# A convolution summed in PSUM, and comparison tables in PSUM

## The chip, the cores and the metric

The kernel runs on one core of a Trainium2 chip. The number is the device time of one execution in microseconds. Five engines work side by side, each through its own queue in order: PE (matrix multiply; its weight loads are listed as PEld), DVE (vector), ACT (activations), POOL (GpSimd), and SP, which here only issues DMAs. SBUF is the working memory. [...]

## The reference, cut to what matters

The input is one sequence of 512 tokens of width 1024. Block one has a mixer and an FFN, block two has attention branches, a cross attention and a product-key expert layer. The change touches the mixer and the expert layer's routing:

```python
# mixer: stick-breaking attention over 8 heads of 64, and beside it
c = glu_a * jax.nn.sigmoid(glu_b)
c = causal_depthwise_conv(c, conv_dw_w[layer], conv_dw_b[layer])   # 31 taps, 512 channels
c = jax.nn.silu(layer_norm(c, conv_ln_g[layer], conv_ln_b[layer]))
mixed = jnp.concatenate([attn, c], axis=-1) @ w_out[layer]
```

In the expert layer each token takes, for each of 8 heads, the 16 best of 128 x 128 expert pairs (i, j) from two lists of 128 keys. With a softmax over the 16 scores as weights w, the output is the weighted sum over the chosen experts of gelu(x . u) v.

## The kernel before, in words

Activations lie transposed, features on partitions and 512 tokens along the free dimension. Weights stream from HBM in chunks of 128 x 1024 (class `Stream`, L47): SP loads one, ACT rounds it to `whi` (L70), POOL subtracts to get `wlo` (L74), and `mm3` (L134) multiplies three times, hi x hi, hi x lo and lo x hi. This POOL subtraction runs through the whole kernel.

**Mixer (L300).** PE's order is written by hand (L498 to L514); a planner places the instructions of the other engines. In iteration j PE does a GEMM of `fills` (24 matmuls), then the `rest` of the fill before it (L430: column sums `misc`, of which DVE's L162 and others make the norm; L415: a transpose of V). From j = 7 it adds the scores `z` of one unit (L449, then a mask, L450, for each of two heads) and the `tail` of the unit before (L479), which needs `sbe` and `splo` from DVE (L459, L466). `weigh` (L485) follows each fourth unit. The depthwise convolution is done by DVE tap by tap (`conv_steps`, L375) in the background: 27 taps for each of four channel blocks, three further taps go to ACT and POOL. `self.bg(TAPS)` places five of them per iteration, `self.bg(TAPS0)` four in the first ones. Then come the layer norm and silu of the convolution (L533 to L558), beside the first half of the output projection. The PSUM banks are: 2 for `mm`, 4 for `z`, 1 `misc`, 1 `av`.

**Routing (L1273).** For 16 key blocks PE makes queries and scores `psc`, from which DVE takes the best 16 (L1285 to L1289). Then, for each 128 tokens, `choose` (L1338) picks the 16 best pairs and looks their keys up (`pick`, L1328). For three of the four token blocks `gates` (L1422) turns that into a 128 x 128 table of weights per token: `onehots` (L1406) compares the column numbers `iota` with i and j for four tokens, J on DVE (L1411), two columns of I on DVE and scaled by ACT (L1416), two compared and scaled in one DVE instruction each (L1418). PE multiplies J and I to `pg` (L1439), and ACT copies that out. Three calls are made ahead (AHEAD). Between such steps PE works on expert blocks (`stored_block`, L1481, 24 matmuls of 384 columns), in an order set by the costs that the generators yield; POOL also gathers rows for the first 128 tokens (L1234), of which DVE takes products (L1248). The PSUM banks are: 2 `mm`, 1 `tr`, 5 `psc`/`pg`. The last stage, `combine` (L1486), sums the experts.

Of the kernel before, what the change touches and what calls it, by code (L numbers as in the profile page):

```python
# [30 lines left out]
TAPS = 5  # L31
# [64 lines left out]
class Kernel:  # L96
# [58 lines left out]
    def rsq(self, out, ss, scale, eps, work, const=1.0, n=512, parts=P, tags=("rsq_y", "rsq_t"), bufs=1):  # L155

        nc = self.nc
        y = work.tile([P, 512], F32, name="rsq_y", tag=tags[0], bufs=bufs)[:parts, :n]
        t = work.tile([P, 512], F32, name="rsq_t", tag=tags[1], bufs=bufs)[:parts, :n]
# [140 lines left out]
    def mixer(self):  # L300
        tc, nc, a = self.tc, self.nc, self.a
        g1 = self.g["norm1_g"]
        with tc.tile_pool(name="mx", bufs=1) as mp, tc.tile_pool(name="mxp", bufs=1, space=PSUM) as pp:
# [8 lines left out]
            nlnb = mp.tile([P, 4], F32, name="nlnb")  # L312
            nc.vector.tensor_scalar(nlnb, lnb, -1.0, None, op0=ALU.mult)
# [46 lines left out]
            def conv_steps(cb):  # L360

                c = conv[:, cb, :]
# [14 lines left out]
                if OFF:  # L377
                    nc.vector.tensor_tensor(c, c, acc, op=ALU.add)
# [63 lines left out]
            def score(b, sb):  # L442
# [42 lines left out]
            def weigh(b):  # L485
                av = pp.tile([P, S], F32, name="av", tag="av", bufs=1)
# [11 lines left out]
            with tc.manual_schedule(engines={mybir.EngineType.PE}):  # L498
                for j in range(FIRST + len(units)):
                    after = fills[j][0](*fills[j][1:]) if j < len(fills) else None  # L500
                    if rest:
                        rest()
                    rest, i = after, j - FIRST
                    if i < -1:
                        self.bg(TAPS0)
                        continue
# [26 lines left out]
            pm = pp.tile([P, S], F32, name="misc", tag="misc", bufs=1)  # L533
# [4 lines left out]
            for cb in range(4):  # L538
# [3 lines left out]
                if cb == 0:  # L542
                    pv = pp.tile([P, S], F32, name="misc", tag="misc", bufs=1)
# [729 lines left out]
    def route(self, ep, rp, pp):  # L1273
# [3 lines left out]
        iota = rp.tile([P, P], F32, name="iota")  # L1277
        nc.gpsimd.iota(iota, pattern=[[1, P]], base=0, channel_multiplier=0, allow_small_or_imprecise_dtypes=True)
# [13 lines left out]
        for b in range(16):  # L1292
            ps = self.gemm("pq", self.xg)
            if b == 0:
                pr = pp.tile([P, S], F32, name="tr", tag="tr", bufs=1)
                self.sums(pr, [self.ssq], self.ones)
                self.rsq(self.rstd, pr, 1.0 / D, EPS, rp, tags=("ut", "ut"), bufs=AHEAD + 1)
            q = rp.tile([P, S], F32, name="pq", tag="pq", bufs=AHEAD + 1)
            nc.vector.tensor_tensor(q, ps, self.rstd, op=ALU.mult)
            pc = pp.tile([P, 4, P], F32, name="psc", tag="psc", bufs=5)  # L1300
# [4 lines left out]
            if b < 8:  # L1305
                t = rp.tile([P, S], F32, name="ut", tag="ut", bufs=AHEAD + 1)
# [31 lines left out]
        def choose(tb):  # L1338
# [59 lines left out]
            pt = pp.tile([P, 3, P], F32, name="tr", tag="tr", bufs=1)  # L1398
# [3 lines left out]
            nc.vector.tensor_copy(t, pt)  # L1402
            T[tb] = t
# [297 lines left out]
```

## Time and profile before

| | us |
|---|---|
| median of 3 runs (lowest, highest) | 2563.18 (2561.69, 2563.8) |
| the profiled execution, its span | 2565.2, 2563.4 |
| PE busy | 2429.5 (95%) |
| DVE busy | 2003.0 (78%) |
| POOL busy, of that the subtraction L74 | 1403.1 (55%), 802.1 at 2548 ns |
| ACT busy | 1071.8 (42%) |

Busy times of one engine are the sum of its instructions. A PE instruction overlaps with the next, so a PE that is busy all the time can still run at the lower of its two clocks; the column PEclk gives the granted share of full speed. "A <- B" in a table of waits says that A stood idle until B was done.

### The profile page before, as it was taken

How to read it: one execution, taken by the hardware profiler on the slowest of the kernel's cores; microseconds unless marked ns; L12 is line 12 of the kernel's file. 1: busy time of each engine (PE TensorE's matmuls, PEld its weight loads, DVE VectorE, ACT ScalarE, POOL GpSimd, SP SyncE). 2: the span in 40 equal slices, each digit the busy share in tenths (PEclk: the TensorE clock that was granted, in tenths of full speed). 3: DMA queues.
4: the chain of work that ended last, by engine and by line, in shares of the span. 5: the costliest groups of instructions: out<-in, count | busy, mean ns of one | idle time of the engine just before them, and what ended most of it. 6: DMA issues, size and time to landing. Idle time of an engine off the chain costs nothing.

```text
span 2563.4 us, 32798 instructions
## 1 busy us (share of the span) xinstructions
PE 2429.5 (95%) x11857; PEld 2038.7 (80%) x11857; DVE 2003.0 (78%) x3144; ACT 1071.8 (42%) x1837; POOL 1403.1 (55%) x714
## 2 busy tenths in 40 slices
PE   7999999999898999999997888989999999999998
PEld 5666788888776767887787888989888888888887
DVE  7978777731457564265999999995999989999995
ACT  4456422232455575435222546554333333333333
POOL 4331444444542313542336455647888888788883
PEclk9899999999999999999999999999999999999999
DMA  4110332233321302332235567779999989898983
GB/s 133 50 50 25 100 99 94 95 97 93 103 91 60 98 26 66 99 107 66 70 100 190 181 224 260 271 257 336 324 318 328 318 293 325 316 319 316 323 301 133
DMA packets 178673, 451.96 MB, mean 176 GB/s; under 512 B 16480, under 2 KB 83200, under 8 KB 175312
## 3 DMA queue, kind: packets, MB, share of 16 engines
q1 hardware_dynamic: 129616, 299.07, 35.0%
q0 software_dynamic: 37232, 135.07, 14.9%
q10 hardware_dynamic: 11664, 15.74, 1.7%
q8 instruction: 93, 1.52, 0.2%
q14 instruction: 68, 0.56, 0.1%
HBM read 409.98 MB, written 39.85 MB: 175 GB/s over the span
## 4 chain that ended last, share of the span: by engine, by line
PE 37%; DVE 20%; issue 6%; POOL 3%; DMA 3%; ACT 2%; SPq 0%; DVEq 0%; POOLq 0%; ACTq 0%
PE acc L1558 12%; PE mm L138 6%; PE mm L137 6%; PE mm L136 6%; DVE I L1418 2%; DVE J L1411 2%; DVE gscr L1248 2%; POOL wlo L74 2%; DVE gacc L1259 1%; DVE I L1411 1%; POOL grow L1234 1%; DMA wraw<-in_peer_u 1%; DVE tmp L1333 1%; PE av L1005 1%; PE tr L659 1%
## 5 line engine op out<-in xcount | busy, mean ns | idle before, releaser
L74 POOL TENSOR_TENSOR wlo<-wraw,whi 128x1024 fp32r<-128x1024 f32 (+1 forms) x315 | 802.1, 2548 | 900.4 <-ACT whi L70 838.4
L70 ACT ACTIVATE whi<-wraw 128x1024 fp32r<-128x1024 f32 (+1 forms) x319 | 333.1, 1046 | 460.8 <-PE mm L137 302.3
L136 PE MATMUL mm<-xhi,whi 128*128 128x512 f32 (+1 forms) x968 | 390.0, 403 | 2.6 <-ACT whi L70 1.2
L138 PE MATMUL mm<-xhi,wlo 128*128 128x512 f32 (+1 forms) x968 | 384.9, 398 | 1.2 <-POOL wlo L74 1.1
L137 PE MATMUL mm<-xlo,whi 128*128 128x512 f32 (+1 forms) x968 | 384.1, 397 | 0.0
L136 PE MATMUL mm<-ushi,whi 128*128 128x384 f32 x1024 | 350.0, 342 | 16.1 <-ACT act L119 16.1
L138 PE MATMUL mm<-ushi,wlo 128*128 128x384 f32 x1024 | 346.5, 338 | 3.7 <-POOL wlo L74 3.7
L137 PE MATMUL mm<-uslo,whi 128*128 128x384 f32 x1024 | 345.7, 338 | 0.0
L1558 PE MATMUL acc<-vl,gahi 128*128 128x512 f32 x768 | 301.9, 393 | 8.1 <-DVE vl L1538 8.1
L1558 PE MATMUL acc<-vh,galo 128*128 128x512 f32 x768 | 301.9, 393 | 1.3 <-DVE galo L192 1.3
L1558 PE MATMUL acc<-vh,gahi 128*128 128x512 f32 x768 | 300.4, 391 | 0.0
L191 ACT ACTIVATE gahi<-gg 128x384 fp32r<-128x384 f32 x128 | 67.3, 526 | 498.5 <-DVE gg L1543 442.4
L1538 POOL TENSOR_TENSOR vl<-vraw,vh 128x1024 fp32r<-128x1024 f32 x85 | 234.7, 2761 | 64.9 <-ACT vh L1537 61.0
L1259 DVE SCALAR_TENSOR_TENSOR gacc<-grow,gw,gacc 128x1024 f32<-128x1024 f32 x128 | 231.4, 1807 | 3.5 <-DMA grow<-in_peer_v,gidx 2.2
L136 PEld LDWEIGHTS mm<-xhi,whi 128*128 128x128 f32 (+1 forms) x968 | 184.3, 190 | 44.3 <-issue 5.9
L137 PEld LDWEIGHTS mm<-xlo,whi 128*128 128x128 f32 (+1 forms) x968 | 184.1, 190 | 40.7 <-issue 3.4
L138 PEld LDWEIGHTS mm<-xhi,wlo 128*128 128x128 f32 (+1 forms) x968 | 183.9, 190 | 40.4 <-POOL wlo L74 1.9
L136 PEld LDWEIGHTS mm<-ushi,whi 128*128 128x128 f32 x1024 | 194.9, 190 | 20.2 <-ACT act L119 17.7
L1234 POOL DMA_INDIRECT grow<-in_peer_ur,gidx x128 | 162.1, 1267 | 86.4 <-PE pg L1439 39.0
L1248 DVE SCALAR_TENSOR_TENSOR gscr<-grow,xr 128x1024 bf16<-128x1024 f32 x128 | 200.7, 1568 | 1.1
L138 PEld LDWEIGHTS mm<-ushi,wlo 128*128 128x128 f32 x1024 | 194.4, 190 | 5.3 <-POOL wlo L74 5.3
L137 PEld LDWEIGHTS mm<-uslo,whi 128*128 128x128 f32 x1024 | 194.9, 190 | 2.4
(426 smaller groups left out, 4679.6 us busy)
## 6 DMA issues: line engine op xcount, KB each, us to landing
wraw<-in_peer_u SPq DMA_DIRECT2D x128, 512.0 KB, 4.6
vraw<-in_peer_v SPq DMA_DIRECT2D x128, 512.0 KB, 6.4
Gd<-stg SPq DMA_DIRECT2D x24, 1024.0 KB, 8.1
rgat<-Gd SPq DMA_DIRECT2D x32, 768.0 KB, 9.6
wraw<-in_w_up SPq DMA_DIRECT2D x44, 512.0 KB, 3.5
Ad<-act ACTq DMA_DIRECT2D x64, 192.0 KB, 3.3
ract<-Ad SPq DMA_DIRECT2D x64, 192.0 KB, 6.6
wraw<-in_w_in SPq DMA_DIRECT2D x20, 512.0 KB, 3.5
```

Source lines behind the costliest of these rows:

```text
L70: self.nc.scalar.activation(hi[:, :w], raw[:, :w], AF.Copy)
L74: self.last_split = self.nc.gpsimd.tensor_tensor(lo[:, :w], raw[:, :w], hi[:, :w].bitcast(F32), op=ALU.subtract)
L136: mm(ps, w[0], x[0], start=start, stop=False)
L137: mm(ps, w[0], x[1], start=False, stop=False)
L138: mm(ps, w[1], x[0], start=False, stop=stop)
L191: self.nc.scalar.activation(hi, src, AF.Copy)
L1234: nc.gpsimd.indirect_dma_start(out=t, out_offset=None, in_=tab.rearrange("a b d -> (a b) d"), in_offset=bass.IndirectOffsetOnAxis(ap=self. ...
L1248: nc.vector.scalar_tensor_tensor(scr, rows.pop(k - lag), 1.0, self.xr, op0=ALU.mult, op1=ALU.mult, accum_out=self.gact[:, k - lag:k - lag ...
L1259: nc.vector.scalar_tensor_tensor(self.gacc, rows.pop(k - lag), self.gw[:, k - lag:k - lag + 1], self.gacc, op0=ALU.mult, op1=ALU.add)
L1411: nc.vector.tensor_tensor(o[:, :n], iota[:, None, :].to_broadcast([P, n, P]), t[:, c, x0:x0 + n, None].to_broadcast([P, n, P]), op=ALU.is_ ...
L1538: ins = (nc.gpsimd if i % 3 else nc.vector).tensor_tensor(vl[:, i % 4, :], r, vh[:, i % 4, :].bitcast(F32), op=ALU.subtract)
L1558: mm(acc[tb][h], x[:, ts], v[:, i % 4, ds], start=False, stop=(i == P - 1 and x is lo), skip_group_check=True)
```

## The change

In the mixer, a convolution block is summed in a PSUM bank `cv` and only its last addition goes to SBUF. `av` gives up its bank and uses `misc`; the layer norm's sums use `cv`. Six taps per iteration replace five. The two score matmuls stand together, the two masks behind them. From j = 7 the `rest` of a fill follows the tail. Silu is one activation instead of three and a multiply. In the routing, one PSUM bank holds `iota`, `first`, and the weights of two token blocks; the look-up source of `pick` lies in the fourth part of the `tr` tile. A call of `onehots` compares I and J in one instruction and scales the two remaining columns of I in another. `psc`/`pg` has four banks instead of five. The SBUF buffers of queries, J and I become one buffer `oh`, which also serves as scratch in the first normalisation.

```diff
-TAPS = 5
+TAPS = 6
...
             def conv_steps(cb):
-                c = conv[:, cb, :]
+                c = pp.tile([P, S], F32, name="cv", tag="cv", bufs=1)
...
                 if OFF:
-                    nc.vector.tensor_tensor(c, c, acc, op=ALU.add)
+                    nc.vector.tensor_tensor(conv[:, cb, :], c, acc, op=ALU.add)
...
                     nc.tensor.matmul(z[:, s, :n], k[hs, t0:t0 + P], q[hs, t0:], start=True, stop=False)
+                for s in range(2):
                     nc.tensor.matmul(z[:, s, :P], identb, maskb, start=False, stop=True)
...
             def weigh(b):
-                av = pp.tile([P, S], F32, name="av", tag="av", bufs=1)
+                av = pp.tile([P, S], F32, name="misc", tag="misc", bufs=1)
...
                     after = fills[j][0](*fills[j][1:]) if j < len(fills) else None
-                    if rest:
-                        rest()
-                    rest, i = after, j - FIRST
+                    i = j - FIRST
                     if i < -1:
+                        if rest:
+                            rest()
+                        rest = after
                         self.bg(TAPS0)
                         continue
...
                     if i >= 0:
                         tail(*units[i])
+                    if rest:
+                        rest()
+                    rest = after
                 weigh(3)
...
-            pm = pp.tile([P, S], F32, name="misc", tag="misc", bufs=1)
+            pm = pp.tile([P, S], F32, name="cv", tag="cv", bufs=1)
...
-                self.act(sg, conv[:, cb, :], AF.Exp, scale=-1.0, bias=nlnb[:, cb:cb + 1])
-                self.act(sg, sg, AF.Ln, bias=1.0)
-                self.act(sg, sg, AF.Exp, scale=-1.0)
-                nc.vector.scalar_tensor_tensor(conv[:, cb, :], conv[:, cb, :], lnb[:, cb:cb + 1], sg,
-                                               op0=ALU.add, op1=ALU.mult)
+                self.act(conv[:, cb, :], conv[:, cb, :], AF.Silu, bias=lnb[:, cb:cb + 1])
...
+        tables = pp.tile([P, 3 * P + 16], F32, name="tables", tag="tables", bufs=1)
+        iota, first = tables[:, :P], tables[:, 3 * P:]
+        nc.vector.tensor_copy(iota, iota_s)
...
-            pc = pp.tile([P, 4, P], F32, name="psc", tag="psc", bufs=5)
+            pc = pp.tile([P, 4, P], F32, name="psc", tag="psc", bufs=4)
...
+            pt = pp.tile([P, 4, P], F32, name="tr", tag="tr", bufs=1)
+            src = pt[:, 3].rearrange("p (h k) -> p h k", k=16)
+            nc.vector.tensor_copy(src[:, :, 0:1], iv[:, :, 0, 0:1])
+            nc.vector.tensor_tensor(src[:, :, 1:], iv[:, :, 0, 1:], iv[:, :, 0, :15], op=ALU.subtract)
...
-            pick(ijw[:, 0], di, pf, first, ALU.is_ge, tmp)
+            pick(ijw[:, 0], src, pf, first, ALU.is_ge, tmp)
             yield 6.6
-            pick(ijw[:, 1], iv[:, :, 1, :], bf, iota[:, :16], ALU.is_equal, tmp)
+            nc.vector.tensor_copy(src, iv[:, :, 1, :])
+            pick(ijw[:, 1], src, bf, iota[:, :16], ALU.is_equal, tmp)
...
+            wp = tables[:, (1 + tb % 2) * P:(2 + tb % 2) * P]
+            nc.vector.tensor_copy(wp, t[:, 2])
...
-        def onehots(t, x0):
-
-            J = rp.tile([P, 4, P], F32, name="J", tag="pq", bufs=AHEAD + 1)
-            I = rp.tile([P, 4, P], F32, name="I", tag="ut", bufs=AHEAD + 1)
-            for o, c, n in ((J, 1, 4), (I, 0, NA)):
-                nc.vector.tensor_tensor(o[:, :n], iota[:, None, :].to_broadcast([P, n, P]),
-                                        t[:, c, x0:x0 + n, None].to_broadcast([P, n, P]), op=ALU.is_equal)
-            for c in range(4):
-                w = t[:, 2, x0 + c:x0 + c + 1]
-                if c < NA:
-                    nc.scalar.activation(I[:, c], I[:, c], AF.Copy, scale=w)
-                else:
-                    self.last_gate = nc.vector.tensor_scalar(I[:, c], iota, t[:, 0, x0 + c:x0 + c + 1], w,
-                                                             op0=ALU.is_equal, op1=ALU.mult)
+        def onehots(t, wp, x0):
+
+            oh = rp.tile([P, 2, 4, P], F32, name="oh", tag="oh", bufs=AHEAD + 1)
+            nc.vector.tensor_tensor(oh, iota[:, None, None, :].to_broadcast([P, 2, 4, P]),
+                                    t[:, 0:2, x0:x0 + 4, None].to_broadcast([P, 2, 4, P]), op=ALU.is_equal)
+            I, J = oh[:, 0], oh[:, 1]
+            for c in range(NA):
+                nc.scalar.activation(I[:, c], I[:, c], AF.Copy, scale=t[:, 2, x0 + c:x0 + c + 1])
+            self.last_gate = nc.vector.tensor_tensor(I[:, NA:], I[:, NA:], wp[:, x0 + NA:x0 + 4, None]
+                                                     .to_broadcast([P, 4 - NA, P]), op=ALU.mult)
             return J, I
```

## Rows read from the trace of the kernel before

**Rows 1.** The chain that ended last, shares of the span by engine (page).

```profile
PE 37%; DVE 20%; issue 6%; POOL 3%; DMA 3%; ACT 2%; SPq 0%; DVEq 0%; POOLq 0%; ACTq 0%
```

**Rows 2.** Busy by stage: bounds, length, PE PEld DVE ACT POOL (instructions), PEclk, DMA.

```profile
28.00:152.00 124.00, 110.77 (x453) 78.67 (x452) 117.72 (x132) 57.71 (x86) 48.56 (x23) 0.92 0.19 60
152.00:262.00 110.00, 102.50 (x445) 69.47 (x444) 80.75 (x99) 61.76 (x91) 26.53 (x13) 0.97 0.14 43
1320.00:1408.00 88.00, 71.16 (x393) 69.28 (x391) 87.21 (x282) 27.32 (x36) 49.45 (x23) 0.94 0.54 177
1408.00:1632.00 224.00, 198.15 (x1239) 194.50 (x1239) 221.71 (x400) 119.44 (x250) 125.25 (x61) 0.96 0.67 231
1632.00:1722.00 90.00, 80.82 (x557) 78.80 (x557) 89.90 (x167) 57.18 (x133) 43.95 (x21) 1.00 0.69 241
1765.00:2556.00 791.00, 781.61 (x3748) 686.28 (x3747) 736.87 (x608) 270.89 (x392) 650.36 (x349) 0.99 0.87 303
```

**Rows 3.** PE's waits, 28-205 us and (last) 205-262: total, times, longest.

```profile
PE misc L188 <- DVE rsq_t L162: 8.5, 2, 5.7
PE z L479 <- DVE splo L466: 2.9, 4, 0.9
PE misc L188 <- ACT qsq L428: 2.5, 1, 2.5
...
PE mm L136 <- DVE xT L528: 2.2, 2, 1.9
```

**Rows 4.** By source line, 375 and 459: ns min/median/max, first, last start.

```profile
L375 DVE SCALAR_TENSOR_TENSOR conv<-cpad,dw,conv x108: 732/748/2889, 37.7 to 222.6; 128x512 f32<-128x512 f32 x108
...
L459 DVE SCALAR_TENSOR_TENSOR sbe<-z,sbe x12: 672/946/1223, 91.7 to 227.1; 128x512 f32<-128x512 f32 x4, 128x768 f32<-128x768 f32 x4, 128x1024 f32<-128x1024 f32 x4
```

**Rows 5.** Line 375 alone: stretch, length, DVE busy (instructions), PEclk, DMA.

```profile
28.00:152.00 124.00, 82.83 (x74) 0.92 0.19 60
```

**Rows 6.** Timeline 42 to 49 us, DVE and POOL: start, duration, instruction.

```profile
42.58 5.17 DVE L375 SCALAR_TENSOR_TENSOR conv<-cpad,dw,conv 128x512 f32<-128x512 f32 x2
47.67 0.68 DVE L162 SCALAR_TENSOR_TENSOR rsq_t<-misc,rsq_y 128x512 f32<-128x512 f32 x1
...
44.86 2.34 POOL L74 TENSOR_TENSOR wlo<-wraw,whi 128x1024 fp32r<-128x1024 f32 x1 [0.58 <-ACT whi L70]
```

**Rows 7.** Timeline of PE: a score pair (192 us), the weighing (208 us).

```profile
192.41 1.12 PE L449 MATMUL z<-qn,qn 64*128 64x512 f32 x2
...
193.62 1.12 PE L449 MATMUL z<-qn,qn 64*128 64x512 f32 x2
...
208.65 2.38 PE L489 MATMUL av<-w,V 128*64 128x512 f32 x16
```

**Rows 8.** Groups by line, 0 to 260 us: busy us, mean ns, idle before.

```profile
L556 DVE SCALAR_TENSOR_TENSOR conv<-conv,lnb,lsg 128x512 f32<-128x512 f32 x4 | 5.0, 1277 | 0.0
...
L116 ACT ACT_TABLE_LOAD x1 | 1.3, 1283 | 0.0
```

**Rows 9.** PE's waits, 1408 to 1722 us: total, times, longest.

```profile
PE pg L1439 <- ACT I L1416: 26.7, 15, 8.9
PE mm L136 <- ACT act L119: 9.6, 4, 4.0
```

**Rows 10.** Groups of DVE by line, 1300 to 1740 us: busy us, mean ns.

```profile
L1418 DVE TENSOR_SCALAR I<-iota,ijwT 128x128 f32<-128x128 f32 x192 | 103.8, 579 | 0.0
L1411 DVE TENSOR_TENSOR J<-iota,ijwT 128x512 f32<-128x512 f32 x96 | 79.4, 828 | 1.8 <-PE pg L1439 1.8
...
L1411 DVE TENSOR_TENSOR I<-iota,ijwT 128x256 f32<-128x256 f32 x96 | 52.6, 548 | 0.0
```

**Rows 11.** By source line, 1411 and 1418: duration ns min/median/max.

```profile
L1411 DVE TENSOR_TENSOR J<-iota,ijwT x96: 672/679/2883, 1408.5 to 1713.1; 128x512 f32<-128x512 f32 x96
L1411 DVE TENSOR_TENSOR I<-iota,ijwT x96: 406/411/2639, 1409.1 to 1713.7; 128x256 f32<-128x256 f32 x96
...
L1418 DVE TENSOR_SCALAR I<-iota,ijwT x192: 285/335/5481, 1409.4 to 1714.3; 128x128 f32<-128x128 f32 x192
```

More of the change, by code (lines that the diff above doesn't have):

```diff
@@ L153, in gemm, with rsq @@
         return ps
-    def rsq(self, out, ss, scale, eps, work, const=1.0, n=512, parts=P, tags=("rsq_y", "rsq_t"), bufs=1):
+    def rsq(self, out, ss, scale, eps, work, const=1.0, n=512, parts=P, tags=("rsq_y", "rsq_t"), bufs=1,
+            yt=None):
         nc = self.nc
-        y = work.tile([P, 512], F32, name="rsq_y", tag=tags[0], bufs=bufs)[:parts, :n]
-        t = work.tile([P, 512], F32, name="rsq_t", tag=tags[1], bufs=bufs)[:parts, :n]
+        if yt is None:
+            yt = [work.tile([P, 512], F32, name="rsq", tag=tag, bufs=bufs)[:parts, :n] for tag in tags]
+        y, t = yt
         self.act(y, ss, AF.Ln, bias=self.eps_t[:parts], scale=scale)
@@ L377, in conv_steps @@
                 if OFF:
-                    nc.vector.tensor_tensor(c, c, acc, op=ALU.add)
+                    nc.vector.tensor_tensor(conv[:, cb, :], c, acc, op=ALU.add)
+                else:
+                    nc.vector.tensor_copy(conv[:, cb, :], c)
                 yield
@@ L542, in mixer @@
                 if cb == 0:
-                    pv = pp.tile([P, S], F32, name="misc", tag="misc", bufs=1)
+                    pv = pp.tile([P, S], F32, name="cv", tag="cv", bufs=1)
                 nc.tensor.matmul(pv, self.ones, sq, start=(cb == 0), stop=(cb == 3))
@@ L1276, in route @@
         nc.sync.dma_start(sk, a["peer_sk"])
-        iota = rp.tile([P, P], F32, name="iota")
-        nc.gpsimd.iota(iota, pattern=[[1, P]], base=0, channel_multiplier=0, allow_small_or_imprecise_dtypes=True)
+        iota_s = rp.tile([P, P], F32, name="iota", tag="tables")
+        nc.gpsimd.iota(iota_s, pattern=[[1, P]], base=0, channel_multiplier=0, allow_small_or_imprecise_dtypes=True)
+        tables = pp.tile([P, 3 * P + 16], F32, name="tables", tag="tables", bufs=1)
+        iota, first = tables[:, :P], tables[:, 3 * P:]
+        nc.vector.tensor_copy(iota, iota_s)
         tv = rp.tile([P, 4, 16, 16], F32, name="tv")
@@ L1296, in route @@
                 self.sums(pr, [self.ssq], self.ones)
-                self.rsq(self.rstd, pr, 1.0 / D, EPS, rp, tags=("ut", "ut"), bufs=AHEAD + 1)
-            q = rp.tile([P, S], F32, name="pq", tag="pq", bufs=AHEAD + 1)
+                yt = rp.tile([P, 2, S], F32, name="yt", tag="oh", bufs=AHEAD + 1)
+                self.rsq(self.rstd, pr, 1.0 / D, EPS, rp, yt=(yt[:, 0], yt[:, 1]))
+            qt = rp.tile([P, 2, S], F32, name="pq", tag="oh", bufs=AHEAD + 1)
+            q = qt[:, 0]
             nc.vector.tensor_tensor(q, ps, self.rstd, op=ALU.mult)
-            pc = pp.tile([P, 4, P], F32, name="psc", tag="psc", bufs=5)
+            pc = pp.tile([P, 4, P], F32, name="psc", tag="psc", bufs=4)
             for tb in range(4):
@@ L1320, in route @@
         NC = 64
-        first = rp.tile([P, 16], F32, name="first")
+        first_s = rp.tile([P, 16], F32, name="first")
         c0 = 0
         for a0, a1, w in rects:
-            nc.gpsimd.iota(first[:, a0:a1], pattern=[[w, a1 - a0]], base=c0, channel_multiplier=0,
+            nc.gpsimd.iota(first_s[:, a0:a1], pattern=[[w, a1 - a0]], base=c0, channel_multiplier=0,
                            allow_small_or_imprecise_dtypes=True)
             c0 += (a1 - a0) * w
+        nc.vector.tensor_copy(first, first_s)
         def pick(dst, src, sel, table, op, tmp):
@@ L1401, in choose @@
             t = rp.tile([P, 3, P], F32, name="ijwT", tag="ijwT", bufs=2)
-            nc.vector.tensor_copy(t, pt)
-            T[tb] = t
+            nc.vector.tensor_copy(t, pt[:, :3])
+            wp = tables[:, (1 + tb % 2) * P:(2 + tb % 2) * P]
+            nc.vector.tensor_copy(wp, t[:, 2])
+            T[tb] = t, wp
             yield 1.0
-        def onehots(t, x0):
-            J = rp.tile([P, 4, P], F32, name="J", tag="pq", bufs=AHEAD + 1)
-            I = rp.tile([P, 4, P], F32, name="I", tag="ut", bufs=AHEAD + 1)
-            for o, c, n in ((J, 1, 4), (I, 0, NA)):
-                nc.vector.tensor_tensor(o[:, :n], iota[:, None, :].to_broadcast([P, n, P]),
-                                        t[:, c, x0:x0 + n, None].to_broadcast([P, n, P]), op=ALU.is_equal)
-            for c in range(4):
-                w = t[:, 2, x0 + c:x0 + c + 1]
-                if c < NA:
-                    nc.scalar.activation(I[:, c], I[:, c], AF.Copy, scale=w)
-                else:
-                    self.last_gate = nc.vector.tensor_scalar(I[:, c], iota, t[:, 0, x0 + c:x0 + c + 1], w,
-                                                             op0=ALU.is_equal, op1=ALU.mult)
+        def onehots(t, wp, x0):
[7 more added lines that the diff above has]
+                                                     .to_broadcast([P, 4 - NA, P]), op=ALU.mult)
             return J, I
         def gates(tb):
-            t = T.pop(tb)
+            t, wp = T.pop(tb)
             oh = {}
             for x in range(0, 4 * AHEAD, 4):
-                oh[x] = onehots(t, x)
+                oh[x] = onehots(t, wp, x)
                 yield 1.2
@@ L1434, in gates @@
                     if x + 4 * AHEAD < P:
[L1435 removed]
+                        oh[x + 4 * AHEAD] = onehots(t, wp, x + 4 * AHEAD)
                     J, I = oh.pop(x)
[L1437 removed]
+                    pg = pp.tile([P, 4, P], F32, name="pg", tag="psc", bufs=4)
                     for c in range(4):
```

11 lines of the change are left out of this document (1 added, 10 removed).

## The prediction, written before the changed kernel ran

> **What bounds the kernel now.** I read the chain by engine first [rows 1]: PE leads with 37%, but DVE has 20% of it, so there are places where the vector engine sets the end. The table by stage says where [rows 2]. In the last stage (1765 to 2556 us) PE is busy 781.6 of 791 us and the change touches nothing there. In three stages that the change does touch, DVE is busy nearly without a break and PE is not: 28 to 152 us (the mixer's first half, DVE 117.7 of 124, PE 110.8), 1408 to 1632 (DVE 221.7 of 224, PE 198.2), and 1632 to 1722 (DVE 89.9 of 90, PE 80.8). In 1320 to 1408 (the first two choices of the routing) it is the same. From 152 to 262 PE leads again, with 7.5 us of waits. [...]
>
> Then I asked why DVE is so full. A tap of the convolution takes 748 ns in the median and up to 2889, and the sum over the PSUM scores z, an instruction of the same kind, never more than 1223 for twice the columns [rows 4]. One place shows the reason [rows 6]: two taps last 5.17 us while POOL's 2.34 us split runs, and PE's next column sum, which needs the PSUM bank that L162 reads behind them, waits 5.7 us, the longest of the 8.5 in [rows 3]. In this trace, a DVE instruction whose inputs all come from SBUF stretches where a POOL tensor operation is in flight; one that takes an input from PSUM doesn't. The tables compare the same way: J takes 679 ns in the median and up to 2883, I up to 2639, and the scaled compare 335 and up to 5481 [rows 11].
>
> **The change, part by part.**
> Taps into PSUM. In 28 to 152 us 74 taps take 82.8 us [rows 5]; at 748 ns they would take 55.4, so 27.5 us are waiting. The trace has no DVE write into PSUM. Nearest rows: a PSUM input costs nothing (z with 512 columns 672 ns at least [rows 4], the compare from SBUF 672 as well [rows 11]), and the worst that I admit is a second cycle per element, 512 x 1.04 = 0.53 us more per tap, with 1.04 ns from J and I: (672 - 406) / 256. In the other direction the z row would let a tap fall from 748 to 672. I take 748 and no extra, as the z row is the nearest.
> [...]
>
> TAPS 5 to 6. Seven iterations before 152 us issue one tap more, 7 x 0.66 = 4.6 us of DVE work moved forward from where DVE has slack (80.8 of 110). DVE then needs 124 - 27.5 + 4.6 = 101 us for this stretch.
>
> The rest behind the tail. Each q/k column sum now comes after the scores and the tail, so it no longer stands in front of them waiting for the evacuated qkt or for the bank: the waits of 8.5 and 2.5 [rows 3] mostly go. (The 5.7 one lies before this order begins, and shrinks with the taps' stretching.) What is late next is the tail's own wait for the split, 2.9 us [rows 3]. Behind a waiting sum on PE's queue stands the next GEMM; behind DVE's L162 stand the taps.
>
> The score pair. Two 64-row matmuls (head halves on partitions 0 to 63 and 64 to 127, separate banks) now stand next to each other, with the masks after both. Before, the first runs from 192.41, its mask follows, and the second starts at 193.62 [rows 7]: 1.05 us each without the mask. The other split shows what neighbours in different halves of the array do: the sixteen `av` matmuls pass 5120 columns in 2.38 us, 0.46 ns each, against 1.05 us / 1024 = 1.03 ns here. If the row halves overlap as those column halves do, each pair saves up to the second one: 1.05 us x (512 + 384 + 256 + 128) / 512 = 2.6 us for each of four head blocks, 10.5 us of PE; if not, 0. I take the overlap.
> [...] No row here shows row halves side by side. [...]
>
> Sum for 28 to 152: PE could be through in 124 - 13.2 (waits) - 9.9 (clock) - 5.2 (half the pairs) = 96 us, DVE in 101. DVE is the later: at most -23, and since its work comes in bursts I take -18. For 152 to 262 PE decides: 5.2 from pairs and half of 7.5 + 3.3 us, -9 (rounded down).
>
> `av` in the bank `misc`. The weighing now needs that bank free, and the next sum waits for ACT's and DVE's split of it. Some 2 us of scores and tail lie between. Bounds: 0, and three times the 5.7 us of the worst bank wait [rows 3]; I take +2.
>
> Silu for Exp, Ln, Exp and a multiply. It drops 8 ACT passes and four DVE instructions of 1277 ns and adds a table load, and another one back for the FFN's Ln, 1283 ns each [rows 8]. It lies beside the first half of the output projection, where PE waited 2.2 us for xT [rows 3]; I count 0. Without that cover the loads would cost 2.6 us.
>
> Tables in PSUM. A call makes J, I and two scaled columns now: on average 828 + 548 + 2 x 579 ns [rows 10]. At the medians 679, 411 and 335 [rows 11] the waiting is 96 x 0.149 + 96 x 0.137 + 192 x 0.244 = 74 us. The new pair, a compare over 1024 columns and a product over 256, has medians of about 1220 (z, 1024 columns [rows 4]) and 411 ns, 1631 against 679 + 411 + 670 = 1760; instructions overlap by some 0.08 us each, so two instead of four are a draw. What goes is the 74 us. A repeated (broadcast) operand in PSUM isn't in the trace; bounds as for the tap, 0 and 1280 x 1.04 = 1.33 us per call; I take 0. Nine copies of at most 128 columns (tables, weights, look-up sources) come in, each below the 411 ns of 256 columns: 2 us, at most 3.7, off the relief; the picks' products lose their stretches too, left out of the sum.
>
> From 1408 to 1722 DVE then needs 312 - 74 + 2 = 240 us and PE 314 - 35 (waits) - 9 (clock) = 270: PE becomes the bound, at most -44. PE's waits there are for ACT's scaled I (26.7), and for the mm buffer that ACT's act frees (9.6) [rows 9], and ACT stands behind DVE in both. The first call after a choice keeps its latency, and DVE still stretches in gscr and the choices; I take two thirds, -29. For 1320 to 1408 the work of the choices hardly changes: between 0 and the 16.8 us of PE's waits, I take -4.
> One PSUM buffer less for pg (5 to 4): +2 for a late evacuation; bounds 0 and a third of the 15 waits for I over again, 5 x 1.8 = 9 us.
>
> Sum: -18 - 9 + 2 - 29 - 4 + 2 = -56. The profiled execution took 2565.2 us, so 2509; it lies 2.0 above the median shown, 2563.2, which gives 2507. I say 2508.
>
> **The rivals.**
> PE gets it all: DVE falls so far behind that no wait and no clock loss stays: -23 - 16 (all of 7.5 + 3.3 + 5.2) - 44 - 10 = -93, 2472. For it: DVE's 240 against PE's 270. Against: the first half of the mixer stays DVE-bound, and gates follow choices directly.
> The waiting moves: POOL's splits stay, and the DVE instructions that still take two SBUF inputs (gscr, the normalisations, the choices) meet them instead. If half comes back, the mixer's DVE needs 115 us (-9), the later half gives -6, and the routing's DVE 277, above PE's 270 (-18): -33 + 4, 2536. (Of the 37 us that DVE then gives in the routing I count half, as its bursts are longer.) For it: POOL is busy for over half of that stage, 125 of 224 us [rows 2]. Against: the table operations are the bulk of DVE's work there, 236 of 312 us [rows 10].
> Slower: an operand in PSUM that is written in place or read repeatedly costs two cycles per element. A tap then takes 0.748 + 0.53 = 1.28 us, where 82.8 / 74 = 1.12 are taken now: 74 x 0.16 = +12 where DVE is late; a call 1.33 - 0.77 more, 96 x 0.56 = +54, all in a stage that DVE bounds; the pairs give -8. That is 2623. It decides from 0.77 us per call on (74 / 96). Against: z streams from PSUM at full rate [rows 4].
> No effect: the stretch comes from something other than the inputs' place: 2563.
>
> **How the numbers follow.** Forecast 0.55 (own range 2490 to 2526), all of it 0.13, moved waits 0.20, no effect 0.04, slower 0.08. Range 2470 to 2548, leaving the slower case, the no-effect case and the far ends of the others out. 0.2% (5 us) is about what a measurement can tell from no change: faster 0.88, same 0.04, slower 0.08.
>
> **What would show it.** Right: taps at 0.75 us with no maximum above 1; the compare over 1024 columns near 1.22; both halves of a 512-column z pair done in about 1.1 us; PE's waits for ACT I below 10 us; the stage from 1408 under 285 us long; the clock above 0.97 in the mixer. Wrong: taps above 1.2 us, or a last stage that grows.

## The result, and the profile after

The changed kernel takes 2477.6 us in the median of four runs (2476.7 to 2479.5), the one before 2563.5 (2561.7 to 2565.1): ratio 0.967, 95% interval 0.965 to 0.968. The profiled execution took 2479.5 us, its span 2477.7. It is 86 us faster where 56 were forecast: inside the whole range (2470 to 2548), but below the 2490 to 2526 that the forecast named as its own.

Three lines of the page after (the span, the busy times, the shares of the chain that ended last):

```profile
span 2477.7 us, 32547 instructions
...
PE 2393.0 (97%) x11857; PEld 2019.8 (82%) x11857; DVE 1909.8 (77%) x2956; ACT 1070.7 (43%) x1831; POOL 1364.8 (55%) x714
...
PE 43%; DVE 13%; issue 6%; POOL 3%; DMA 3%; ACT 2%; DVEq 0%; SPq 0%; POOLq 0%; ACTq 0%
```

PE's share of the chain rose from 37% to 43%, DVE's fell from 20% to 13% [rows 1]. Where the time went is read from the first starts of four kinds of matmul, which both kernels make in the same order (by source line: ns min/median/max, first and last start):

```profile
L136 PE MATMUL mm<-chi,whi x32: 392/393/469, 231.5 to 253.9; 128*128 128x512 f32 x32
...
L1310 PE MATMUL psc<-sk,pq x128: 272/275/377, 1182.8 to 1281.2; 128*128 128x128 f32 x128
...
L1447 PE MATMUL pg<-oh x768: 272/275/582, 1365.3 to 1634.7; 128*128 128x128 f32 x192
...
L1572 PE MATMUL acc<-ident,xT x48: 275/275/377, 1636.0 to 1641.3; 128*128 128x128 f32 x48
```

They cut the span into stages. The same cut for every kernel in this study, from its profiled execution (us):

| kernel | mixer, to the first chi product | to the first psc | queries, to the last psc | choices, to the first pg | gates, to the first acc | to the end | median of the runs | ratio to before, 95% interval |
|---|---|---|---|---|---|---|---|---|
| before | 259.4 | 954.4 | 103.7 | 92.5 | 310.6 | 842.8 | 2563.5 | |
| after | 231.5 | 951.3 | 98.4 | 84.1 | 270.7 | 841.7 | 2477.6 | 0.965 to 0.968 |
| tables_in_sbuf | 228.6 | 950.5 | 98.4 | 84.1 | 308.1 | 839.5 | 2513.7 | 0.979 to 0.983 |
| conv_in_sbuf | 260.1 | 953.0 | 98.4 | 84.2 | 270.7 | 841.5 | 2510.3 | 0.978 to 0.981 |
| pair_alone | 255.3 | 952.7 | 104.7 | 92.4 | 310.2 | 843.0 | 2562.9 | 0.999 to 1.001 |
| no_pool_split | 231.9 | 954.0 | 104.9 | 72.1 | 266.5 | 830.4 | 2458.8 | 0.957 to 0.960 |
| pairs_undone | 234.2 | 953.9 | 98.4 | 84.6 | 271.5 | 841.3 | 2483.5 | 0.967 to 0.970 |
| rest_first | 233.9 | 951.0 | 98.4 | 84.1 | 270.7 | 841.8 | 2481.7 | 0.966 to 0.969 |
| taps5 | 235.9 | 954.4 | 98.4 | 84.1 | 270.7 | 842.0 | 2485.1 | 0.968 to 0.971 |
| one_buffer | 260.0 | 953.2 | 98.4 | 93.3 | 311.1 | 843.3 | 2557.3 | 0.996 to 0.998 |
| silu_undone | 229.0 | 951.0 | 98.4 | 84.1 | 270.7 | 841.7 | 2480.5 | 0.967 to 0.969 |
| rsq_in_psum | 225.4 | 949.8 | 99.9 | 84.0 | 270.6 | 839.5 | 2471.1 | 0.963 to 0.966 |
| rsq_taps7 | 223.3 | 944.8 | 99.9 | 84.8 | 271.7 | 841.7 | 2468.1 | 0.962 to 0.964 |
| rsq_and_block | 223.8 | 947.1 | 99.9 | 92.6 | 264.1 | 841.4 | 2473.6 | 0.964 to 0.967 |

After and tables_in_sbuf have the same mixer and differ by 2.9 us there, so differences below about 3 us in one profile's mixer tell nothing; in the second column all kernels but two lie within 5 us. The gain stands in the mixer (-27.9), the queries (-5.3), the choices (-8.4) and the gates (-39.9). The engines in these stages of after (stretch, length, PE, PEld, DVE, ACT, POOL busy, PEclk, DMA, GB/s):

```profile
28.00:106.60 78.60, 74.23 (x336) 56.50 (x335) 71.85 (x95) 42.89 (x64) 34.56 (x18) 0.98 0.23 80
106.60:189.90 83.30, 80.58 (x410) 57.67 (x410) 72.44 (x98) 53.92 (x80) 26.14 (x13) 0.98 0.16 51
189.90:231.50 41.60, 36.81 (x144) 24.63 (x141) 24.84 (x33) 20.94 (x27) 7.26 (x3) 0.92 0.10 34
...
1281.20:1365.30 84.10, 72.28 (x408) 71.33 (x406) 82.81 (x307) 27.86 (x38) 45.51 (x24) 0.97 0.56 186
1365.30:1636.00 270.70, 266.01 (x1783) 264.93 (x1783) 253.63 (x375) 176.79 (x381) 142.25 (x81) 0.99 0.77 273
```

In the gates PE is busy 266.0 of 270.7 us, and DVE has 17 us to spare: PE sets the length now, where DVE did in [rows 2]. PSUM is the memory that PE's matmuls write; DVE and ACT read it in both traces, and in after DVE also writes it. The instructions that moved there, by source line in after, answer to [rows 4, 11]:

```profile
L375 DVE SCALAR_TENSOR_TENSOR cv<-cpad,dw,cv x108: 736/756/756, 37.8 to 193.4; 128x512 f32<-128x512 f32 x108
...
L1421 DVE TENSOR_TENSOR oh<-tables,ijwT x96: 1204/1216/1226, 1363.6 to 1627.6; 128x1024 f32<-128x1024 f32 x96
...
L1426 DVE TENSOR_TENSOR oh<-oh,tables x96: 393/420/422, 1365.0 to 1628.9; 128x256 f32<-128x256 f32 x96
```

Median and maximum lie within 10 ns of each other now; before, the maximum of a tap was 2889. And PE's waits from 1365 to 1636 us of after, where [rows 9] has 26.7 us for ACT's I alone:

```profile
PE pg L1447 <- ACT oh L1425: 9.2, 3, 5.8
PE acc L1572 <- ACT stg L1448: 1.0, 1, 1.0
PE mm L136 <- ACT act L119: 0.2, 1, 0.2
```

How the stretch works is seen in a few microseconds of after. First POOL's timeline (the second of the two splits from 40.96 also by itself), then DVE's (start, length):

```profile
40.96 5.30 POOL L74 TENSOR_TENSOR wlo<-wraw,whi 128x1024 fp32r<-128x1024 f32 x2
43.42 2.84 POOL L74 TENSOR_TENSOR wlo<-wraw,whi 128x1024 fp32r<-128x1024 f32 x1
...
50.36 2.40 POOL L74 TENSOR_TENSOR wlo<-wraw,whi 128x1024 fp32r<-128x1024 f32 x1 [4.09 <-ACT whi L70]
```

```profile
42.66 0.74 DVE L375 SCALAR_TENSOR_TENSOR cv<-cpad,dw,cv 128x512 f32<-128x512 f32 x1
43.31 0.68 DVE L165 SCALAR_TENSOR_TENSOR rsq<-rsq 128x512 f32<-128x512 f32 x1
...
44.57 2.24 DVE L166 SCALAR_TENSOR_TENSOR rr<-rsq 128x512 f32<-128x512 f32 x1
46.74 0.74 DVE L375 SCALAR_TENSOR_TENSOR cv<-cpad,dw,cv 128x512 f32<-128x512 f32 x1
...
51.23 2.07 DVE L165 SCALAR_TENSOR_TENSOR rsq<-rsq 128x512 f32<-128x512 f32 x1
```

POOL's splits run to 46.26 and to 52.76. The tap at 42.66, with one input from PSUM, begins beside a split and takes its 0.74 us. L166 and L165 take both inputs from SBUF; the two that begin beside a split end at 46.81 and 53.30, some 0.55 us behind it. The wait goes the other way too: the L165 at 43.31 began 0.11 us before the second split and takes its 0.68 us, and that split takes 2.84 where the one at 50.36 takes 2.40.

These few lines stand for the whole. In the trace of before, all 22 taps that begin while a POOL tensor operation is in flight end 0.55 to 0.56 us behind it; in after 37 begin like that, and none takes more than 756 ns. Of POOL's splits of 1024 columns in before up to 235 us, 15 begin with a DVE instruction on SBUF inputs alone in flight; they take 2.64 us in the median, the 8 others 2.35 to 2.40.

### The profile page after: what moved, and what is told of

Same layout as the page of the kernel before. It is cut to its first block, busy times and chain, and to the rows that moved or that the text cites. A ratio compares the mean times of both kernels' runs of the same rounds, so it can differ in the third digit from the quotient of the medians.

```text
span 2477.7 us, 32547 instructions
## 1 busy us (share of the span) xinstructions
PE 2393.0 (97%) x11857; PEld 2019.8 (82%) x11857; DVE 1909.8 (77%) x2956; ACT 1070.7 (43%) x1831; POOL 1364.8 (55%) x714
## 4 chain that ended last, share of the span: by engine, by line
PE 43%; DVE 13%; issue 6%; POOL 3%; DMA 3%; ACT 2%; DVEq 0%; SPq 0%; POOLq 0%; ACTq 0%
PE acc L1566 11%; PE mm L138 8%; PE mm L137 8%; PE mm L136 8%; PE pg L1447 3%; DVE gscr L1250 1%; POOL grow L1236 1%; POOL wlo L74 1%; DVE gacc L1261 1%; DVE gg L1551 1%; DMA grow<-in_peer_v,gidx 1%; DMA vraw<-in_peer_v 1%; PE av L1007 1%; PE tr L661 1%; DVE galo L194 1%
## 5 line engine op out<-in xcount | busy, mean ns | idle before, releaser
L74 POOL TENSOR_TENSOR wlo<-wraw,whi 128x1024 fp32r<-128x1024 f32 (+1 forms) x315 | 776.8, 2467 | 853.3 <-ACT whi L70 792.7
L1261 DVE SCALAR_TENSOR_TENSOR gacc<-grow,gw,gacc 128x1024 f32<-128x1024 f32 x128 | 237.2, 1853 | 2.9 <-DMA grow<-in_peer_v,gidx 1.6
L1250 DVE SCALAR_TENSOR_TENSOR gscr<-grow,xr 128x1024 bf16<-128x1024 f32 x128 | 218.1, 1704 | 1.1
L1236 POOL DMA_INDIRECT grow<-in_peer_ur,gidx x128 | 152.3, 1190 | 87.9 <-DVE gscr L1250 48.7
```

What stands on the lines that cost most here:

```text
L74: self.last_split = self.nc.gpsimd.tensor_tensor(lo[:, :w], raw[:, :w], hi[:, :w].bitcast(F32), op=ALU.subtract)
L1236: nc.gpsimd.indirect_dma_start(out=t, out_offset=None, in_=tab.rearrange("a b d -> (a b) d"), in_offset=bass.IndirectOffsetOnAxis(ap=self. ...
L1250: nc.vector.scalar_tensor_tensor(scr, rows.pop(k - lag), 1.0, self.xr, op0=ALU.mult, op1=ALU.mult, accum_out=self.gact[:, k - lag:k - lag ...
L1261: nc.vector.scalar_tensor_tensor(self.gacc, rows.pop(k - lag), self.gw[:, k - lag:k - lag + 1], self.gacc, op0=ALU.mult, op1=ALU.add)
```

## The experiments

**Does the place do it?** Theory: a DVE instruction with two SBUF inputs stretches beside POOL's split, and PSUM takes the taps and tables out of it. Rival: fewer instructions, the order and the pairs made the gain. Two runs undo the place alone, one takes the split away and leaves the place.

```diff
# tables_in_sbuf, from after
-            nc.vector.tensor_tensor(oh, iota[:, None, None, :].to_broadcast([P, 2, 4, P]),
+            nc.vector.tensor_tensor(oh, iota_s[:, None, None, :].to_broadcast([P, 2, 4, P]),
...
-            self.last_gate = nc.vector.tensor_tensor(I[:, NA:], I[:, NA:], wp[:, x0 + NA:x0 + 4, None]
+            self.last_gate = nc.vector.tensor_tensor(I[:, NA:], I[:, NA:], t[:, 2, x0 + NA:x0 + 4, None]
```

> The kernel after, but the compare takes iota from SBUF and the product takes the weights from SBUF; shapes and instruction count stay. Theory (a DVE instruction with two SBUF inputs stretches beside POOL): the compare's mean rises from 1216 to 1500-1900 ns with a maximum above 3000, the stage from the first pg to the combine grows from 271 to 295-325 us, the whole to 2500-2530. Rival (two instructions in place of four made the gain): compare at 1220, stage within 275, whole 2476-2482.

By source line, and the stage of the gates:

```profile
L1421 DVE TENSOR_TENSOR oh<-iota,ijwT x96: 1206/1214/3429, 1359.9 to 1662.5; 128x1024 f32<-128x1024 f32 x96
...
L1426 DVE TENSOR_TENSOR oh<-oh,ijwT x96: 366/413/2626, 1362.2 to 1663.8; 128x256 f32<-128x256 f32 x96
```

```profile
1361.60:1669.70 308.10, 283.77 (x1783) 276.60 (x1783) 291.49 (x372) 176.68 (x381) 167.54 (x81) 0.95 0.68 239
```

The median is that of PSUM, the maximum is back, and the compare's mean is 1544 ns, as the theory has it. The stage is 308.1 us again: of its 39.9 us the place of the tables holds 37.4, everything else in it 2.5. The widths show what a waiting instruction does: the compares over 1024 columns that wait for a split end 1.08 to 1.12 us behind it, the products over 256 columns 0.28 to 0.29.

```diff
# conv_in_sbuf, from after
-                c = pp.tile([P, S], F32, name="cv", tag="cv", bufs=1)
+                c = conv[:, cb, :]
```

> The kernel after, but the taps accumulate in SBUF again; order, pairs and TAPS stay. Theory: taps back at 950-1100 ns in the mean, first product with chi 12-25 us later than 231.5, whole 2490-2503. Rival (order and pairs made the mixer's gain): taps longer but no more than 6 us of the whole, 2478-2484.

```profile
L375 DVE SCALAR_TENSOR_TENSOR conv<-cpad,dw,conv x108: 732/750/2890, 37.3 to 222.9; 128x512 f32<-128x512 f32 x108
```

The taps are busy 107.2 us, 993 ns each, and the mixer takes 260.1 us, as long as before. Order, pairs, six taps and Silu together show no gain in the mixer while the taps stretch; the mixer is 28.6 us longer than in after, where 12 to 25 were expected.

```diff
# no_pool_split, from before
...
-        self.nc.scalar.activation(hi[:, :w], raw[:, :w], AF.Copy)
-        if self.chunks[i][0] in self.on_vector and i % 2:
...
+        ins = self.nc.scalar.activation(hi[:, :w], raw[:, :w], AF.Copy)
+        if self.chunks[i][0] in ("w_in", "u"):
+            lo, self.last_split = hi, ins
+        elif self.chunks[i][0] in self.on_vector and i % 2:
```

> The kernel before with POOL's split left out for the chunks of w_in and u (their low part is replaced by the rounded weight, so these products are not the reference's); the taps and tables stay in SBUF. Theory (POOL's split is what stretches them): taps 740-780 ns in the mean with no maximum above 1300, J at 680, the scaled compare at 335-350; mixer and routing shorten by about what the change brings, whole 2470-2505. Rival (an accumulation in place in SBUF, or the place alone, is slow): taps stay above 1000 ns, whole 2545-2565.

```profile
L378 DVE SCALAR_TENSOR_TENSOR conv<-cpad,dw,conv x108: 734/744/2884, 32.6 to 194.2; 128x512 f32<-128x512 f32 x108
...
L1414 DVE TENSOR_TENSOR J<-iota,ijwT x96: 671/684/734, 1361.4 to 1620.5; 128x512 f32<-128x512 f32 x96
...
L1421 DVE TENSOR_SCALAR I<-iota,ijwT x192: 327/341/353, 1362.3 to 1621.7; 128x128 f32<-128x128 f32 x192
```

With all operands in SBUF, the tables lose every stretch and the mixer and gates are as short as after (231.9, 266.5). The taps keep some: they take 90.5 us, 838 ns each with a maximum of 2884, against 740 to 780 and 1300 expected. The ten that begin beside POOL's other work (the gated product, the adds of the other three taps, the splits of w_out) end 0.55 us behind it as before. Mixer and gates gain alike from either side, POOL's or the operand's; that settles the cause. A matmul that no longer waits for `wlo` doesn't explain it: from 1408 to 1722 us of before these waits are 1.4 us in all, and from 28 to 260 there are none. The whole is below the 2470 to 2505 expected, since the choices (72.1) and the last stage (830.4), where chunks of u pass without a split as well, are 12 and 11 us shorter than in after; why is not shown.

**What are the other edits worth?** pair_alone is before with only the masks moved behind both products; pairs_undone is after with each mask behind its own product.

> The kernel before with the two score matmuls side by side and the masks behind, nothing else. Theory (row halves overlap, but the first half of the mixer stays bound by DVE): PE busy in the scores from 26.9 to 12-13 us, of which 4-9 us reach the whole: 2554-2560. Rival one (all of it reaches the end): 2548-2551. Rival two (the overlap pays nothing as long as DVE is late): 2561-2565.

> The kernel after with each mask behind its own score matmul again; the rest stays. Theory (with the taps in PSUM, PE sets the mixer, so the pairs' time reaches the end now, where alone it did not): PE busy in the scores from 12.5 to 24-27 us, first product with chi at 239-244 instead of 231.5, whole 2485-2490. Rival (the pairs don't reach the end here either): at most 3 us, 2476-2481.

A 512-column pair in the timeline of after, against [rows 7], and what the scores cost PE in after, pair_alone and pairs_undone (the window 28 to 235 for this line alone: length, PE and PEld busy, PEclk, DMA, GB/s):

```profile
125.28 1.13 PE L451 MATMUL z<-qn,qn 64*128 64x512 f32 x4
126.35 0.28 PE L453 MATMUL z<-maskb,identb 128*128 128x128 bf16 x2
```

```profile
28.00:235.00 207.00, 12.96 (x64) 4.82 (x64) 0.97 0.17 59
```

```profile
28.00:235.00 207.00, 13.70 (x64) 5.02 (x64) 0.94 0.16 51
```

```profile
28.00:235.00 207.00, 25.69 (x64) 9.42 (x64) 0.99 0.18 59
```

Both halves now take 1.13 us together where one took 1.12: the row halves run at the same time, and PE is spared 12.7 us. Little of it arrives. On its own the pair shows nothing in the whole (ratio 0.999 to 1.001; 4.1 us in the mixer of its profile), which is rival two and fits a mixer that waits for DVE. In after, undoing it costs 2.7 us in the mixer and 5.9 between the medians, with overlapping intervals: less than the theory has, more than the rival. What became of the rest is read from 28 us to the mark in pairs_undone, in after, and in tables_in_sbuf, which runs the same mixer as after (length, PE, PEld, DVE, ACT, POOL busy, PEclk, DMA, GB/s):

```profile
28.00:234.20 206.20, 198.96 (x886) 140.65 (x885) 170.19 (x225) 117.82 (x169) 67.50 (x34) 0.99 0.18 58
```

```profile
28.00:231.50 203.50, 191.62 (x884) 138.80 (x884) 169.14 (x225) 117.75 (x169) 67.96 (x34) 0.97 0.17 59
```

```profile
28.00:228.60 200.60, 188.74 (x885) 136.35 (x884) 169.02 (x225) 117.61 (x169) 68.00 (x34) 0.98 0.19 59
```

With the overlap PE stands idle 11.9 us in either execution, without it 7.2: some 4.6 of the 12.7 us turn into gaps. The mixer is 2.7 us shorter in the one and 5.6 in the other. For the remainder the granted clock is lower with the overlap (0.97 and 0.98 against 0.99). That this is the pairs' doing is not shown: the same mixer has 0.92 from 189.9 us to the mark in after and 1.00 there in tables_in_sbuf.

> The kernel after with the column sums of a fill in front of scores and tail again. Theory: PE waits again for qkt and the bank, 3-8 us more waits in the mixer, whole 2480-2486. Rival (the waits of before came from the stretched taps alone): waits and mark within 2 us, whole 2476-2480.

rest_first puts `rest()` back in front of scores and tail. PE's largest wait from 28 to 260 us in it (total, times, longest):

```profile
PE misc L492 <- DVE rsq L164: 6.2, 2, 3.6
```

L492 is the weighing: it waits for the bank `misc`, which the sum put in front of it still holds until DVE's L164 has read it. After has no such wait for DVE. The last tap starts at 196.9 us instead of 193.4, the whole is 4.2 us longer in the median with overlapping intervals: waits came back, as expected but another one than expected, and their size in the whole is not settled.

> The kernel after with five taps an iteration. Theory: DVE has room, so the last tap comes 8-15 us later than 193.4 and the layer norm of the convolution is late behind the last scores: first product with chi 3-10 us later, whole 2480-2487. Rival (a tap less before 107 us lets PE through earlier): mark 1-4 us earlier, whole 2473-2477.

Last tap at 198.1, 4.7 us later and not 8 to 15; mixer 4.4 us longer, whole 7.6 in the median. Of the single edits this one comes nearest to standing apart (0.968 to 0.971).

> The kernel after with the convolution's Silu as Exp, Ln, Exp and a multiply again. Theory (hidden beside the first half of the output projection): first product with chi within 1 us of 231.5, whole 2475-2480. Rival (the chain of ACT passes is on the path since the convolution ends late): 2-6 us later, whole 2480-2484.

It is 2.9 us slower between the medians, 2.5 us the other way in the mixer of the profile: no effect shown.

**The queries.** No table and no tap is used there, and yet the stage lost 5.3 us in after, in tables_in_sbuf and in conv_in_sbuf. one_buffer is before with the merged buffer alone:

```diff
# one_buffer, from before
...
-            q = rp.tile([P, S], F32, name="pq", tag="pq", bufs=AHEAD + 1)
+            qt = rp.tile([P, 2, S], F32, name="pq", tag="oh", bufs=AHEAD + 1)
+            q = qt[:, 0]
...
-                t = rp.tile([P, S], F32, name="ut", tag="ut", bufs=AHEAD + 1)
+                t = qt[:, 1]
...
-            J = rp.tile([P, 4, P], F32, name="J", tag="pq", bufs=AHEAD + 1)
-            I = rp.tile([P, 4, P], F32, name="I", tag="ut", bufs=AHEAD + 1)
+            oh = rp.tile([P, 2, 4, P], F32, name="oh", tag="oh", bufs=AHEAD + 1)
+            I, J = oh[:, 0], oh[:, 1]
```

> The kernel before with query and expert input, and J and I, as two halves of one buffer oh; five psc banks, tables in SBUF, four instructions a call as before. Theory (the shared buffer ties the two-input product ut to the query, off POOL's split): ut's mean from 1153 to about 735 ns, the stage from the first to the last psc from 103.7 to 98-99 us, whole 2556-2560. Rival (four psc banks or the earlier stages made those 5 us): ut above 1000, stage 103-105, whole 2561-2565.

DVE's groups, 1205 to 1410 us, of before and then of one_buffer (busy us, mean ns):

```profile
L1307 DVE SCALAR_TENSOR_TENSOR ut<-xT,norm_ffn,rstd 128x512 f32<-128x512 f32 x8 | 9.1, 1153 | 0.0
```

```profile
L1308 DVE SCALAR_TENSOR_TENSOR pq<-xT,norm_ffn,rstd 128x512 f32<-128x512 f32 x8 | 5.8, 732 | 0.0
```

The product still has two SBUF inputs; it only comes at another moment, between POOL's splits. In before two of the eight begin beside a split and take 2.08 and 2.74 us; in one_buffer none does, and from the third on they come every 6.7 to 7.2 us. The stage is 98.4 us as in after, and the whole 0.996 to 0.998 of before: a shared buffer paid by the order that it imposes. The product itself gave 3.3 of the 5.3 us (9.1 to 5.8); the other 2 were not traced.

**A faster version.** After still has two-input instructions in the mixer (L165, above). The sum that a normalisation starts from lies in PSUM and isn't needed again, so `t` can be written over it:

```diff
# rsq_in_psum, from after
-        y, t = yt
+        y, t = yt[0], ss
```

> The kernel after; the normalisation's intermediate t is written over its sum in PSUM, so two of its three DVE instructions have one SBUF input less. Theory (the two-SBUF instructions left in the mixer still meet POOL's split): L165 from 1222 to about 750 ns, no maximum above 800 there, 3-6 us of DVE in the mixer, of which 1-4 us reach the end, whole 2473-2477. Rival (PE sets the mixer now, and the longer hold of the bank costs as much): 2476-2481.

By source line:

```profile
L165 DVE SCALAR_TENSOR_TENSOR misc<-misc,rsq x10: 681/692/700, 27.5 to 258.5; 128x512 f32<-128x512 f32 x10
```

The maximum of 2257 that L165 has in after is gone, the mixer takes 225.4 us, the last tap starts at 187.5, and the whole is 2471.1 us (2470.0 to 2473.0), where no run of after is below 2476.7 (the intervals of the ratios overlap a little). It gained a little more than I expected.

> The kernel rsq_in_psum with seven taps an iteration. Theory (with DVE relieved the convolution can end earlier, and its layer norm waits less): last tap 5-10 us before 193.4, wait for conv of 1.8 us gone, whole 2469-2475. Rival (more DVE work in the first half makes PE late there): whole 2477-2485.

2468.1 us, the lowest median but for no_pool_split; its interval overlaps that of rsq_in_psum. The mechanism I gave isn't there: the last tap starts at 186.8 us, only 0.7 earlier than in rsq_in_psum, and the wait for the convolution of 1.8 us, which rsq_in_psum no longer has, is there again.

> The kernel rsq_in_psum with one expert block more between the second choice and the first gates (its step costs 5.1 in place of 1.0). Theory (PE waits 5.8 us for the first scaled I and then runs at the lower clock): that wait goes, the clock of 1360-1380 rises from 0.74, whole 4-8 us below rsq_in_psum. Rival (the order in DVE's queue puts the third choice ahead anyway, so the wait only moves behind the block): within 2 us of rsq_in_psum.

PE's waits from 1330 to 1400 us, of rsq_in_psum and then of rsq_and_block:

```profile
PE pg L1447 <- ACT oh L1425: 8.3, 2, 5.8
PE tr L1410 <- DVE ijw L1343: 1.6, 1, 1.6
```

```profile
PE mm L136 <- ACT act L119: 7.5, 1, 7.5
PE tr L1410 <- DVE ijw L1343: 1.6, 1, 1.6
```

The rival was right: the wait moved, and the whole is 2.5 us longer. PE fills its time with a block, and then a block waits for a buffer that ACT empties, 7.5 us instead of 8.3; the clock of 1360 to 1380 us did rise (0.83 to 0.97), but the choices got 8.6 us longer and the gates 6.5 shorter.

## Why the prediction was right, and where its sizes were off

**The cause** was right: in these traces DVE instructions whose inputs all come from SBUF stretch beside POOL's tensor operations (all 22 taps of before that begin beside one, up to 2889 ns), and a PSUM input takes them out (37 begin so in after, none above 756 ns). In the timeline of after, two instructions with both inputs in SBUF end some 0.55 us behind a split, a tap with one input in PSUM takes its 0.74 us beside one, and the split that began second takes 2.84 us. What in the chip makes them wait for each other is not shown. Two inputs are not the whole of it here: the scaled compare (L1418) takes one tensor and two per-partition scalars from SBUF, and by the prediction's own figures it had 47 of the 74 us of waiting (192 x 0.244). All 11 of them that begin beside a split end 0.08 to 0.09 us behind it. With most of the split away (no_pool_split) its maximum is 353 ns.

**The price of PSUM** taken as none was right: tap 756 ns in the median against 750 in SBUF, compare 1216 against 1214, product 420 against 413. The 1.04 ns more per element, on which the slower rival rests, are not there; written in place and read repeatedly, PSUM costs these instructions at most 7 ns. The first product of each convolution block, which the sum leaves out, did pay: it has one tensor input, and with its output in PSUM it takes 815 ns instead of 540, 1.1 us for all four. Its rows in after and in conv_in_sbuf:

```profile
L363 DVE TENSOR_SCALAR cv<-cpad,dw,dwb x4: 812/815/816, 36.9 to 158.4; 128x512 f32<-128x512 f32 x4
```

```profile
L363 DVE TENSOR_SCALAR conv<-cpad,dw,dwb x4: 534/540/548, 36.7 to 188.2; 128x512 f32<-128x512 f32 x4
```

**28 to 262 us**: -25 forecast, -27.9 measured. That the sum fits so well is partly luck. DVE's last product `ga` (it scales the output of a GEMM) divides the mixer close to 152 us; its rows of before and of after (last start):

```profile
L391 DVE TENSOR_TENSOR ga<-mm,rstd x3: 676/677/685, 52.8 to 152.8; 128x512 f32<-128x512 f32 x3
```

```profile
L393 DVE TENSOR_TENSOR ga<-mm,rstd x3: 676/681/681, 48.7 to 126.2; 128x512 f32<-128x512 f32 x3
```

Up to there 26.6 us are gained (24.7 in tables_in_sbuf, with the same mixer), where -18 was taken and -23 called the most; behind it 1.3 (6.1) are, where -9 + 2 was taken. So the reserve for DVE's bursts was too large, as in the gates, and the later half gave less than its sum. The pairs overlap (1.13 us for both halves, 1.12 for one before); their 10.5 us of PE are 12.7. Half of the 10.5 stands in the sum; 2.7 to 5.6 us of mixer arrive in the profiles. The clock, which was to rise above 0.97 in the mixer, is 0.97 there in after and 0.98 in tables_in_sbuf (0.94 in before). The clock terms of the forecast, 9.9 and 3.3 us here and 9 in the gates, are the author's estimates, the share of full clock missing in [rows 2] times the length (0.08 x 124, 0.03 x 110, 0.04 x 224); no run shows what they are worth in time, only that the clock of the gates is 0.99 in after. The +2 for `av` was not needed: in after the waits for DVE to read the bank `misc` are 0.3 us.

**Gates**: -29 + 2 forecast, -39.9 measured. This is the step that failed: "I take two thirds, -29". The bound of -44 was right to 4 us: PE is busy 266.0 us and waits 4.6 more. The reasons for two thirds didn't hold. gscr stretched even more (below, 1647 ns from 1365 to 1636 us; 1370 in before from 1200 to 1740), and DVE needs 254 us where 240 were forecast; but DVE still has 17 us to spare, and PE's waits for I within the stage are 3.4 us. The first call's latency, 5.8 of the 9.2 us, ends at the first `pg` and so falls into the choices. The bank less (+2) cost nothing that shows: no wait for a free `pg` bank is among PE's waits.

**Queries and choices**: -4 forecast, -13.7 measured. The choices were bound by DVE, which is busy 82.8 of 84.1 us even now. I left the picks' products "out of the sum"; their means fell from 3382 and 2802 ns (four each, before) to 2274. Of that some 2 us lie within the choices. Another 4.6 us only moved: the kernel before makes a third compare and product of a first look-up ahead of the first `pg`, and after makes them behind it, where DVE has room. And I costed one buffer in place of two at nothing, without asking what order it imposes: 5.3 us.

**The moved waits** happened: L165's mean in the mixer rose from 1102 to 1222 ns, qn's from 740 to 1148, 4.5 us in all (10 x 0.12 + 8 x 0.41). They are not the only ones. DVE's busy time from 28 us to the mark fell from 197.2 us (below) to 169.1, by 28.1, where the taps alone lost 32.9 and the dropped multiply 5.0: some 10 us came back, 1.1 of it the price of PSUM above. That is a good quarter of the taps' gain, not half. Part of it reached the end, as rsq_in_psum shows. In before:

```profile
28.00:259.40 231.40, 210.71 (x885) 146.00 (x883) 197.19 (x229) 118.56 (x176) 73.48 (x34) 0.94 0.16 51
```

In the end the rival "PE gets it all" (2472) had the better size, though not by its terms: in the mixer it has -39, and waits and clock loss stayed; the gates have -44 and the choices -10, which the text doesn't work out. The groups of DVE in after that these points rest on, two from 28 to 260 us, two from 1365 to 1636 (busy us, mean ns):

```profile
L165 DVE SCALAR_TENSOR_TENSOR rsq<-rsq 128x512 f32<-128x512 f32 x10 | 12.2, 1222 | 0.0
...
L438 DVE SCALAR_TENSOR_TENSOR qn<-qkt,qg,rr 128x512 f32<-128x512 f32 x8 | 9.2, 1148 | 0.0
...
L1250 DVE SCALAR_TENSOR_TENSOR gscr<-grow,xr 128x1024 bf16<-128x1024 f32 x43 | 70.8, 1647 | 0.2
...
L1342 DVE TENSOR_TENSOR tmp<-tmp,tr 128x2048 f32<-128x2048 f32 x4 | 9.1, 2274 | 0.0
```

## What to carry to other kernels

Where a vector instruction's maximum is far above its median (here 2889 against 748 ns), look at what POOL does at that moment, and give the instruction a PSUM input where one is to be had; an accumulator, a small table or a sum that is used up anyway did here. Once the stalled engine falls below the next one, take the next engine's full time as the bound and leave out the cautious factor, unless a wait is named that keeps it. A time saved on an engine that isn't late (the pairs, 12.7 us of PE) showed nothing (0.999 to 1.001 in pair_alone) until the late one was relieved, and only a part of it then (2.7 to 5.6 us of mixer).

## What the hardware showed that was not expected

A DVE instruction with its inputs all in SBUF that waits for POOL's split ends behind it by a time that goes with its width and not with the moment it began: in before 0.28 to 0.29 us for 256 columns (six I of L1411), 0.55 to 0.56 for 512 (22 taps), 1.08 to 1.09 for 1024 (16 of L1248). That looks like standing still until the split ends and not like running slower; the traces give only starts and ends. Not all wait: nine other I begin beside a split in before and take 0.41 us, and there the split is the one that is late (3.0 to 4.1 us), as it is when the DVE instruction began first (2.84 us in place of 2.40). Merging two buffers moved an untouched instruction off POOL's split, 1153 to 732 ns. And the granted clock differs between two executions of the same mixer: 0.92 from 189.9 us to the mark in after, 1.00 in tables_in_sbuf, where the mixer is 2.9 us shorter. A difference of that size in one profile is not an edit's.
